# A macaron decoder layer in float32: two weight differences made by adding transfers, three pairs of k tiles by seven products, x in four pieces

## Chip, cores, metric

One core of one Trainium2 chip runs the whole layer for a sequence of 256 positions. The metric is the device time of one execution in microseconds, as a median over runs.

## What is computed

The layer is a feed-forward part, a token mixer (dilated and differential attention with two gates), and a second feed-forward part. The change touches the two feed-forward parts, which are alike:

```python
D_MODEL, SEQ, D_FF = 2048, 256, 5632

def swiglu(h, w_gate, w_up, w_down):
    return (jax.nn.silu(h @ w_gate) * (h @ w_up)) @ w_down

x = x + 0.5 * swiglu(rms_norm(x, ffn1_norm), ffn1_w_gate, ffn1_w_up, ffn1_w_down)
...
x = x + 0.5 * swiglu(rms_norm(x, ffn2_norm), ffn2_w_gate, ffn2_w_up, ffn2_w_down)
```

All inputs are float32, and so is the output.

## The kernel before, in words

**Three matmuls a product.** Every float32 factor is kept as two parts: hi, a rounded copy that ScalarE makes, and lo, the rest, that VectorE makes by a subtraction. A product of two factors is then three matmuls on TensorE: hi with hi, hi with lo, lo with hi (`three`, lines 139 to 144; in `linear`, lines 133 to 135). The activations stand on TensorE as 128 x 128 weights, and 512 columns of the layer's weight matrix stream past.

**From memory to TensorE.** Weights come in tiles of two k tiles by 512 columns (512 KB). SP's queue loads one into a slot `raw` (four slots, pool `wraw`). ScalarE then makes `w_hi` from it and VectorE makes `w_lo`, into one of five pairs of slots (pool `wspl`), to which the feed-forward parts add a sixth (`FFN_SPL`, pool `acth`). A raw slot comes free when both parts are made and no difference still needs it; a hi/lo pair comes free when TensorE has used it. The helper `parts` (line 98) makes both, on lines 102 and 103; `weight_groups` (line 106) does the same on lines 117 and 118 for all other matrices.

**Two chunks at once.** The hidden width of 5632 is cut into 11 chunks of 512 columns. The first is made by `linear`, gate and up one after the other. For each of the other ten, `two_chunks` (line 166) makes gate and up together, walking over eight pairs u of k tiles. For a plain pair it does eight products: two k tiles, two halves of the positions, two matrices. For the pairs in `WINO` (3 and 5) it does seven, by Winograd's form of Strassen's method on 2 x 2 blocks: activations on one side, and on the other b00, b10 (gate's two k tiles) and b01, b11 (up's two). The sums of activations come from `sums_of_x` (line 146), once for each feed-forward part. The differences of weights are made for each pair on VectorE, on lines 203, 204, 209 and 210: b01 - b00, b01 - b11, b11 - (b01 - b00), and b10 less the last. `t_a` and `t_b` hold them, and each is split into hi and lo like a raw tile. Eight PSUM banks hold the four results and the four products.

**After a call.** Adds on VectorE put the results together (lines 220 to 226), ScalarE applies SiLU (line 372), VectorE multiplies and transposes blocks of 32 x 32 (line 267), SP writes the blocks to memory and reads them back in another order (`moved`, line 272), and eight groups later ScalarE and VectorE split them into hi and lo (`ah` and `al`, lines 240 and 241) for the product with w_down.

**What sets the order.** A list `later` holds work to be done after so many groups of weights (`defer`, `tick`). Within that, the compiler's scheduler orders the instructions of each engine by what it thinks is ready; afterwards every engine, and SP's and POOL's queues of transfers, keeps to its order. `tc.issue_after(ins)` puts what follows behind `ins` on its engine.

**At the start.** x is loaded in eight pieces of 256 columns by `load_x` (line 330), each followed by transposes on TensorE and a split; the first chunk's weight tiles come between them. `table_loads` (line 469) brings small tables through POOL's queue: four for the gains of the heads (line 472), four for lambda (line 475), and the positions. It is deferred to group 34. `rsqrt_mean` (line 229) uses a power operation on POOL.

Of the kernel before, what the change touches and what calls it, by code (L numbers as in the profile page):

```python
# [11 lines left out]
F32 = mybir.dt.float32  # L12
# [7 lines left out]
P = 128  # L20
# [12 lines left out]
FFN_SPL = 1  # L33
WINO = (3, 5)
# [19 lines left out]
def hybrid_layer_kernel(ctx: ExitStack, tc: tile.TileContext, a: dict, out: bass.AP):  # L54
# [34 lines left out]
    wtmp = None  # L89
    spl_turn = itertools.count()  # L90
# [7 lines left out]
    def parts(src, n=GRP):  # L98

        nonlocal last_hi, last_lo  # L100
        hi, lo = split_tiles()
        last_hi = nc.scalar.activation(hi[:, :n], src, AF.Copy)  # L102
        last_lo = nc.vector.tensor_tensor(lo[:, :n], src, hi[:, :n].bitcast(F32), op=ALU.subtract)  # L103
        return hi, lo

    def weight_groups(w, n0, nk):

        nonlocal last_hi, last_lo
        for k0 in range(0, nk, GRP):
            raw = wraw.tile([P, GRP, CH], F32, name="raw")  # L110
            hi, lo = split_tiles()
            step = 1 if groups == 0 else GRP
            for g in range(0, GRP, step):
                ks = slice(g, g + step)
                nc.sync.dma_start(raw[:, ks], w[(k0 + g) * P:(k0 + g + step) * P, n0:n0 + CH]
                                  .rearrange("(k p) n -> p k n", p=P))
                last_hi = nc.scalar.activation(hi[:, ks], raw[:, ks], AF.Copy)  # L117
                last_lo = nc.vector.tensor_tensor(lo[:, ks], raw[:, ks], hi[:, ks].bitcast(F32), op=ALU.subtract)  # L118
            yield k0, hi, lo
# [26 lines left out]
    def sums_of_x(pool, pairs):  # L146
# [3 lines left out]
        for u in pairs:  # L150
            f = wtmp.tile([P, GRP, CH], F32, name="t_a")
# [14 lines left out]
    def two_chunks(j, cols, xh, xl, nk, sx, tmp):  # L166
# [15 lines left out]
        for u in range(nu):  # L182
            raw = []
            for w, n0 in cols:
                r = wraw.tile([P, GRP, CH], F32, name="raw")
                nc.sync.dma_start(r, w[2 * u * P:(2 * u + 2) * P, n0:n0 + CH].rearrange("(k p) n -> p k n", p=P))
                raw.append(r)
# [11 lines left out]
            part = lambda hl, k: (hl[0][:, k], hl[1][:, k])  # L199
            b = parts(raw[0])  # L200

            ta, tb = wtmp.tile([P, GRP, CH], F32, name="t_a"), wtmp.tile([P, GRP, CH], F32, name="t_b")
            nc.vector.tensor_tensor(ta[:, 0], raw[1][:, 0], raw[0][:, 0], op=ALU.subtract)
            nc.vector.tensor_tensor(ta[:, 1], raw[1][:, 0], raw[1][:, 1], op=ALU.subtract)
# [4 lines left out]
            nc.vector.tensor_tensor(tb[:, 0], raw[1][:, 1], ta[:, 0], op=ALU.subtract)  # L209
            nc.vector.tensor_tensor(tb[:, 1], raw[0][:, 1], tb[:, 0], op=ALU.subtract)  # L210
            tick()
            b = parts(ta)
            three(p5, sm(0), part(b, 0), st, sp)
            three(p7, sm(2), part(b, 1), st, sp)
            b = parts(tb)
# [12 lines left out]

    def rsqrt_mean(ss, n, cols):

        v = small.tile([P, cols], F32, name=f"rv{cols}")
        nc.vector.tensor_scalar(v, ss, 1.0 / n, EPS, op0=ALU.mult, op1=ALU.add)
        r = small.tile([P, cols], F32, name=f"rr{cols}")
        nc.gpsimd.tensor_tensor(r, v, mhalf[:, :cols], op=ALU.pow)
        return r
# [94 lines left out]
    def load_x(i):  # L330

        if i < KD // 2:
            cols = slice(i * 2 * P, (i + 1) * 2 * P)
            nc.sync.dma_start(xs[:, :, cols], xv[:, :, cols])
            to_kmajor([xs[:, t, cols] for t in range(NT)], xh, xl, 2 * i, g1)
# [11 lines left out]
    def ffn(wg, wu, wd, norm, done, ahead=None):  # L347
        nonlocal wtmp
        with tc.tile_pool(name="act", bufs=1) as apool, tc.tile_pool(name="actw", bufs=1) as aw, \
                tc.tile_pool(name="actb", bufs=1) as bp, tc.tile_pool(name="acts", bufs=1) as sxp, \  # L350
                tc.tile_pool(name="actt", bufs=1) as wt, tc.tile_pool(name="acth", bufs=FFN_SPL) as spl:
            wtmp = wt
            more_spl.append(spl)
# [27 lines left out]
            more_spl.clear()  # L381
# [87 lines left out]
    def table_loads():  # L469

# [374 lines left out]
```

## Time and profile before

| | us |
|---|---|
| median of 3 runs | 2135.52 (2135.37 to 2136.85) |
| the profiled execution | 2133.2 |
| its span, first to last instruction | 2131.4 |

TensorE's clock was granted at 0.999 of full speed on average. The page gives busy times of the engines as shares of the span. Matmuls are pipelined: one matmul's record runs on beside the next one's, so the price of a matmul is the step from one start to the next. Idle time of another engine costs nothing as long as TensorE is fed.

### The profile page before, as it was taken

How to read it: one execution, taken by the hardware profiler on the slowest of the kernel's cores; microseconds unless marked ns; L12 is line 12 of the kernel's file. 1: busy time of each engine (PE TensorE's matmuls, PEld its weight loads, DVE VectorE, ACT ScalarE, POOL GpSimd, SP SyncE). 2: the span in 40 equal slices, each digit the busy share in tenths (PEclk: the TensorE clock that was granted, in tenths of full speed). 3: DMA queues.
4: the chain of work that ended last, by engine and by line, in shares of the span. 5: the costliest groups of instructions: out<-in, count | busy, mean ns of one | idle time of the engine just before them, and what ended most of it. 6: DMA issues, size and time to landing. Idle time of an engine off the chain costs nothing.

```text
span 2131.4 us, 25439 instructions
## 1 busy us (share of the span) xinstructions
PE 2112.3 (99%) x9370; PEld 1744.8 (82%) x9370; DVE 1482.3 (70%) x1880; ACT 1063.4 (50%) x1297; POOL 48.9 (2%) x50
## 2 busy tenths in 40 slices
PE   8999999999999999999999999999999999999999
PEld 7878888888888888888888888888888888888887
DVE  6788864588876665767755556676888745788853
ACT  6454543355545554555555444454554533455532
POOL 0000000000000011011100000000000000000000
PEclk9999999999999999999999999999999999999999
DMA  8666675566677766666654567676766755667673
GB/s 262 199 200 217 225 241 194 168 220 230 212 238 256 237 200 227 228 214 215 196 191 158 185 228 243 226 234 189 228 216 217 254 191 187 198 212 231 228 244 121
DMA packets 241665, 456.26 MB, mean 214 GB/s; under 512 B 14162, under 2 KB 37252, under 8 KB 241284
## 3 DMA queue, kind: packets, MB, share of 16 engines
q1 hardware_dynamic: 241152, 454.09, 64.4%
q0 software_dynamic: 288, 0.53, 0.2%
q8 instruction: 73, 1.20, 0.2%
q14 instruction: 52, 0.43, 0.1%
q10 hardware_dynamic: 100, 0.03, 0.0%
HBM read 428.89 MB, written 25.69 MB: 213 GB/s over the span
## 4 chain that ended last, share of the span: by engine, by line
PE 75%; DVE 11%; DMA 10%; issue 2%; ACT 1%; SPq 0%; DVEq 0%; ACTq 0%
PE mm L133 19%; PE mm L134 19%; PE mm L135 19%; DMA raw<-in_ffn_w_up_dram 7%; DVE w_lo L103 6%; PE mm L143 2%; PE mm L144 2%; PE mm L142 2%; PE tr L143 2%; PE tr L144 2%; PE tr L142 2%; PE s L144 1%; PE s L143 1%; PE s L142 1%; DMA raw<-in_ffn_w_gate_dram 1%
## 5 line engine op out<-in xcount | busy, mean ns | idle before, releaser
L118 DVE TENSOR_TENSOR w_lo<-raw,w_hi 128x1024 fp32r<-128x1024 f32 (+1 forms) x449 | 543.3, 1218 | 379.1 <-ACT w_hi L117 377.2
L117 ACT ACTIVATE w_hi<-raw 128x1024 fp32r<-128x1024 f32 (+1 forms) x449 | 471.4, 1056 | 482.1 <-PE mm L135 400.8
L102 ACT ACTIVATE w_hi<-raw 128x1024 fp32r<-128x1024 f32 x320 | 316.4, 1003 | 222.9 <-DMA raw<-in_ffn_w_gate_dram 47.8
L103 DVE TENSOR_TENSOR w_lo<-raw,w_hi 128x1024 fp32r<-128x1024 f32 x320 | 361.9, 1150 | 71.0 <-ACT w_hi L102 69.7
L133 PE MATMUL mm<-w_hi,xh 128*128 128x512 f32 x864 | 339.4, 394 | 0.0
L134 PE MATMUL mm<-w_lo,xh 128*128 128x512 f32 x864 | 338.9, 393 | 0.0
L135 PE MATMUL mm<-w_hi,xl 128*128 128x512 f32 x864 | 336.4, 392 | 0.0
L133 PE MATMUL mm<-w_hi,ah 128*128 128x512 f32 x704 | 273.9, 389 | 1.8 <-DVE e L226 1.8
L135 PE MATMUL mm<-w_hi,al 128*128 128x512 f32 x704 | 273.9, 389 | 0.0
L134 PE MATMUL mm<-w_lo,ah 128*128 128x512 f32 x704 | 273.9, 389 | 0.0
L143 PE MATMUL mm<-w_lo,xh 128*128 128x512 f32 x540 | 210.6, 390 | 0.3 <-DVE w_lo L103 0.3
L144 PE MATMUL mm<-w_hi,xl 128*128 128x512 f32 x540 | 210.1, 389 | 0.0
L142 PE MATMUL mm<-w_hi,xh 128*128 128x512 f32 x540 | 209.4, 389 | 0.0
L135 PEld LDWEIGHTS mm<-w_hi,xl 128*128 128x128 f32 x864 | 162.6, 188 | 33.6
L134 PEld LDWEIGHTS mm<-w_lo,xh 128*128 128x128 f32 x864 | 162.8, 188 | 33.3
L133 PEld LDWEIGHTS mm<-w_hi,xh 128*128 128x128 f32 x864 | 162.7, 189 | 33.3
L133 PEld LDWEIGHTS mm<-w_hi,ah 128*128 128x128 f32 x704 | 132.2, 188 | 30.0 <-ACT w_hi L117 1.4
L135 PEld LDWEIGHTS mm<-w_hi,al 128*128 128x128 f32 x704 | 132.2, 188 | 27.7
L134 PEld LDWEIGHTS mm<-w_lo,ah 128*128 128x128 f32 x704 | 132.2, 188 | 27.2
L143 PEld LDWEIGHTS mm<-w_lo,xh 128*128 128x128 f32 x540 | 101.4, 188 | 22.9 <-DVE w_lo L103 1.9
L142 PEld LDWEIGHTS mm<-w_hi,xh 128*128 128x128 f32 x540 | 101.4, 188 | 21.1
L144 PEld LDWEIGHTS mm<-w_hi,xl 128*128 128x128 f32 x540 | 101.4, 188 | 20.9
(229 smaller groups left out, 2717.5 us busy)
## 6 DMA issues: line engine op xcount, KB each, us to landing
raw<-in_w_in_dram SPq DMA_DIRECT2D x184, 512.0 KB, 3.6
raw<-in_ffn_w_up_dram SPq DMA_DIRECT2D x176, 512.0 KB, 4.7
raw<-in_ffn_w_down_dram SPq DMA_DIRECT2D x176, 512.0 KB, 4.7
raw<-in_ffn_w_gate_dram SPq DMA_DIRECT2D x175, 512.0 KB, 4.5
blocks<-turned SPq DMA_DIRECT2D x41, 512.0 KB, 4.1
raw<-in_w_out_dram SPq DMA_DIRECT2D x32, 512.0 KB, 4.5
moved<-blocks SPq DMA_DIRECT2D x31, 512.0 KB, 4.7
raw<-in_w_diff_branch_dram SPq DMA_DIRECT2D x16, 512.0 KB, 4.8
```

The costliest lines, as they stand in the source:

```text
L102: last_hi = nc.scalar.activation(hi[:, :n], src, AF.Copy)
L103: last_lo = nc.vector.tensor_tensor(lo[:, :n], src, hi[:, :n].bitcast(F32), op=ALU.subtract)
L117: last_hi = nc.scalar.activation(hi[:, ks], raw[:, ks], AF.Copy)
L118: last_lo = nc.vector.tensor_tensor(lo[:, ks], raw[:, ks], hi[:, ks].bitcast(F32), op=ALU.subtract)
L133: nc.tensor.matmul(ps[t], xh[:, k, sl], hi[:, kk], start=k == 0, stop=False)
L134: nc.tensor.matmul(ps[t], xh[:, k, sl], lo[:, kk], start=False, stop=False)
L135: nc.tensor.matmul(ps[t], xl[:, k, sl], hi[:, kk], start=False, stop=k == nk - 1)
L142: nc.tensor.matmul(ps, h, wh, start=start, stop=False)
L143: nc.tensor.matmul(ps, h, wl, start=False, stop=False)
L144: nc.tensor.matmul(ps, l, wh, start=False, stop=stop)
```

## The change

- `WINO` becomes (2, 4, 5): three pairs of k tiles go by seven products.
- Two of the four weight differences, b01 - b00 and b01 - b11, are made without VectorE. ScalarE writes -b00 and -b11 into `t_a`, and two transfers from POOL's queue add the block b01 from memory in place. The block b01 has no other use, so up's first k tile is no longer loaded into a raw slot for those pairs.
- The other two differences are written over b00 and b10 in the raw slot of gate, whose hi and lo parts have been made by then. `t_b` is gone; `t_a` has two slots.
- The feed-forward parts have a fifth raw slot (`FFN_RAW`) in place of the sixth hi/lo pair. The sums of x use raw slots as scratch.
- x is loaded in four pieces, of 256, 256, 512 and 1024 columns.
- The small tables are loaded behind the latest power operation on POOL.

```diff
-FFN_SPL = 1
-WINO = (3, 5)
+FFN_SPL = 0
+FFN_RAW = 1
+WINO = (2, 4, 5)
...
+    def raw_tile():
+        pool = wraw
+        if more_raw and next(raw_turn) % (RAW_BUFS + FFN_RAW) >= RAW_BUFS:
+            pool = more_raw[0]
+        return pool.tile([P, GRP, CH], F32, name="raw")
...
-            for w, n0 in cols:
-                r = wraw.tile([P, GRP, CH], F32, name="raw")
-                nc.sync.dma_start(r, w[2 * u * P:(2 * u + 2) * P, n0:n0 + CH].rearrange("(k p) n -> p k n", p=P))
+            for i, (w, n0) in enumerate(cols):
+                r = raw_tile()
+                k = i if u in sx else 0
+                nc.sync.dma_start(r[:, k:], w[(2 * u + k) * P:(2 * u + 2) * P, n0:n0 + CH]
+                                  .rearrange("(k p) n -> p k n", p=P))
...
+            b00, b10, b11 = raw[0][:, 0], raw[0][:, 1], raw[1][:, 1]
+            w, n0 = cols[1]
+            ta = wtmp[0].tile([P, GRP, CH], F32, name="t_a")
+            for i, block in enumerate((b00, b11)):
+                nc.scalar.activation(ta[:, i], block, AF.Copy, scale=-1.0)
+                nc.gpsimd.dma_start(ta[:, i], w[2 * u * P:(2 * u + 1) * P, n0:n0 + CH], accum_op=ALU.add)
             b = parts(raw[0])
-
-            ta, tb = wtmp.tile([P, GRP, CH], F32, name="t_a"), wtmp.tile([P, GRP, CH], F32, name="t_b")
-            nc.vector.tensor_tensor(ta[:, 0], raw[1][:, 0], raw[0][:, 0], op=ALU.subtract)
-            nc.vector.tensor_tensor(ta[:, 1], raw[1][:, 0], raw[1][:, 1], op=ALU.subtract)
             three(p1, op(0, 0), part(b, 0), st, sp)
             three(c00, op(1, 0), part(b, 1), False, False)
             b = parts(raw[1][:, 1:], 1)
             three(c01, sm(3), part(b, 0), False, False)
-            nc.vector.tensor_tensor(tb[:, 0], raw[1][:, 1], ta[:, 0], op=ALU.subtract)
-            nc.vector.tensor_tensor(tb[:, 1], raw[0][:, 1], tb[:, 0], op=ALU.subtract)
             tick()
+            nc.vector.tensor_tensor(b00, b11, ta[:, 0], op=ALU.subtract)
+            nc.vector.tensor_tensor(b10, b10, b00, op=ALU.subtract)
             b = parts(ta)
             three(p5, sm(0), part(b, 0), st, sp)
             three(p7, sm(2), part(b, 1), st, sp)
-            b = parts(tb)
+            b = parts(raw[0])
...
         if i < KD // 2:
+            if i in (0, 1, 2, 4):
+                piece = slice(i * 2 * P, max(2 * i, 1) * 2 * P)
+                nc.sync.dma_start(xs[:, :, piece], xv[:, :, piece])
             cols = slice(i * 2 * P, (i + 1) * 2 * P)
-            nc.sync.dma_start(xs[:, :, cols], xv[:, :, cols])
...
     def table_loads():
+        with tc.issue_after(last_pow[-1].ins):
+            small_loads()
+
+    def small_loads():
```

## Rows read from the trace of the kernel before

**Rows 1.** The page: busy time, share of the span and instructions of each engine.
```profile
PE 2112.3 (99%) x9370; PEld 1744.8 (82%) x9370; DVE 1482.3 (70%) x1880; ACT 1063.4 (50%) x1297; POOL 48.9 (2%) x50
```

**Rows 2.** Windows of 50 us: busy by engine, granted clock, DMA share, GB/s.
```profile
core 0: us, PE busy (x) PEld busy (x) DVE busy (x) ACT busy (x) POOL busy (x), PEclk, DMA share, GB/s
0.00:50.00 50.00, 42.54 (x192) 35.00 (x193) 33.11 (x53) 33.38 (x58) 5.02 (x14) 1.00 0.80 260
100.00:150.00 50.00, 46.33 (x197) 37.79 (x196) 43.85 (x86) 27.90 (x33) 0.00 (x0) 0.97 0.66 212
150.00:200.00 50.00, 50.00 (x223) 41.40 (x222) 43.34 (x53) 27.46 (x32) 0.00 (x0) 1.00 0.67 214
200.00:250.00 50.00, 49.58 (x219) 40.53 (x218) 42.27 (x49) 24.53 (x27) 0.00 (x0) 1.00 0.67 221
250.00:300.00 50.00, 49.22 (x216) 39.99 (x215) 39.19 (x43) 26.96 (x30) 0.00 (x0) 1.00 0.73 246
550.00:600.00 50.00, 49.27 (x216) 39.98 (x215) 40.37 (x50) 25.44 (x29) 0.00 (x0) 1.00 0.64 214
1650.00:1700.00 50.00, 48.95 (x216) 40.26 (x215) 40.56 (x44) 26.04 (x29) 0.00 (x0) 1.00 0.74 249
1950.00:2000.00 50.00, 49.35 (x218) 40.29 (x217) 42.31 (x51) 27.24 (x32) 0.00 (x0) 1.00 0.65 212
```

**Rows 3.** Timeline of TensorE, first and last of 85 matmul starts: start, duration.
```profile
149.62 0.39 PE L142 MATMUL mm<-w_hi,xh 128*128 128x512 f32 x1
...
168.66 0.39 PE L142 MATMUL mm<-w_hi,xh 128*128 128x512 f32 x1
```

**Rows 4.** Groups of instructions: count, busy us, mean ns, idle before and its releaser.
```profile
L102 ACT ACTIVATE w_hi<-t_a 128x1024 fp32r<-128x1024 f32 x40 | 42.2, 1055 | 39.5 <-PE s L144 18.9 <-PE mm L144 18.9 <-ACT w_hi L102 1.0
L103 DVE TENSOR_TENSOR w_lo<-t_a,w_hi 128x1024 fp32r<-128x1024 f32 x40 | 48.6, 1215 | 3.7 <-ACT w_hi L102 3.7
L203 DVE TENSOR_TENSOR t_a<-raw 128x512 f32<-128x512 f32 x40 | 27.7, 692 | 82.1 <-DMA raw<-in_ffn_w_up_dram 82.1
L102 ACT ACTIVATE w_hi<-raw 128x512 fp32r<-128x512 f32 x40 | 24.9, 623 | 23.6 <-PE s L144 13.3 <-PE mm L144 9.1 <-DMA raw<-in_ffn_w_up_dram 1.0
...
L153 DVE TENSOR_TENSOR t_a<-xh,xl 128x512 f32<-128x512 f32 x4 | 2.7, 687 | 0.1
```

**Rows 5.** POOL's loads of line 475 (64 KB each): issue in ns, landing.
```profile
L475 POOL DMA_DIRECT2D junk<-in_diff_lq_dram x2: 538/564/589, 87.7 to 89.2; - x2
...
DMA to landing us min/median/max: 4.0/6.1/6.4
```

**Rows 6.** DMA issues: count, KB each, median us from issue to landing.
```profile
raw<-in_ffn_w_up_dram SPq DMA_DIRECT2D x176, 512.0 KB, 4.7
```

**Rows 7.** Timelines of VectorE and TensorE, pair 5 of one call.
```profile
166.13 0.69 DVE L203 TENSOR_TENSOR t_a<-raw 128x512 f32<-128x512 f32 x1 [2.85 <-DMA raw<-in_ffn_w_up_dram]
...
173.76 1.22 DVE L103 TENSOR_TENSOR w_lo<-t_a,w_hi 128x1024 fp32r<-128x1024 f32 x1
...
177.28 0.39 PE L143 MATMUL tr<-w_lo,sx_h 128*128 128x512 f32 x1
```

**Rows 8.** Windows of 10 us, columns as in rows 2.
```profile
0.00:10.00 10.00, 2.54 (x10) 2.10 (x11) 2.02 (x5) 3.15 (x6) 3.73 (x11) 1.00 0.75 218
10.00:20.00 10.00, 10.00 (x43) 8.07 (x43) 6.90 (x10) 6.96 (x11) 0.00 (x0) 1.00 1.07 375
80.00:90.00 10.00, 10.00 (x45) 8.26 (x45) 9.86 (x20) 5.67 (x7) 2.27 (x4) 1.00 0.75 220
```

**Rows 9.** Timeline of POOL: start, duration, and idle before with its releaser.
```profile
1.29 0.71 POOL L472 DMA_DIRECT2D qkg<-in_dil_q_norm_dram  x1 [0.34 <-issue]
...
87.73 0.59 POOL L475 DMA_DIRECT2D junk<-in_diff_lq_dram  x1 [46.57 <-DVE mask L431]
```

**Rows 10.** Timeline of TensorE at the start.
```profile
8.83 1.09 PE L253 MATMUL tr<-ident,xs 128*128 128x128 f32 x4 [3.32 <-DMA xs<-in_x_dram]
9.57 0.78 PE L133 MATMUL mm<-w_hi,xh 128*128 128x512 f32 x1
```

**Rows 11.** Waits: who for whom, us in total, times, longest.
```profile
ACT ah L240 <- DMA moved<-blocks: 107.9, 22, 8.5
...
PE tr L143 <- DVE w_lo L103: 5.2, 4, 3.7
```

More of the change, by code (lines that the diff above doesn't have):

```diff
@@ L88, in hybrid_layer_kernel @@
     more_spl = []
-    wtmp = None
-    spl_turn = itertools.count()
+    more_raw = []
+    wtmp = []
+    spl_turn, raw_turn = itertools.count(), itertools.count()
+    def raw_tile():
[3 more added lines that the diff above has]
+        return pool.tile([P, GRP, CH], F32, name="raw")
     def split_tiles():
@@ L109, in weight_groups @@
         for k0 in range(0, nk, GRP):
-            raw = wraw.tile([P, GRP, CH], F32, name="raw")
+            raw = raw_tile()
             hi, lo = split_tiles()
@@ L150, in sums_of_x @@
         for u in pairs:
-            f = wtmp.tile([P, GRP, CH], F32, name="t_a")
+            f = raw_tile()
             x, sm = f[:, 0].rearrange("p (k s) -> p k s", s=S), f[:, 1].rearrange("p (i m) -> p i m", m=P)
@@ L227, in two_chunks @@
         return (e, x), (u2, y)
+    last_pow = []
     def rsqrt_mean(ss, n, cols):
@@ L233, in rsqrt_mean @@
         r = small.tile([P, cols], F32, name=f"rr{cols}")
-        nc.gpsimd.tensor_tensor(r, v, mhalf[:, :cols], op=ALU.pow)
+        last_pow.append(nc.gpsimd.tensor_tensor(r, v, mhalf[:, :cols], op=ALU.pow))
         return r
@@ L347, in ffn @@
     def ffn(wg, wu, wd, norm, done, ahead=None):
-        nonlocal wtmp
         with tc.tile_pool(name="act", bufs=1) as apool, tc.tile_pool(name="actw", bufs=1) as aw, \
                 tc.tile_pool(name="actb", bufs=1) as bp, tc.tile_pool(name="acts", bufs=1) as sxp, \
-                tc.tile_pool(name="actt", bufs=1) as wt, tc.tile_pool(name="acth", bufs=FFN_SPL) as spl:
-            wtmp = wt
-            more_spl.append(spl)
+                tc.tile_pool(name="actt", bufs=FFN_RAW) as wt, tc.tile_pool(name="acth", bufs=2) as sums:
+            more_raw.append(wt)
+            wtmp.append(sums)
             ah = apool.tile([P, 4 * HALVES[0], S], F32R, name="ah")
@@ L380, in ffn @@
                     (done if half else part)(n, ps, bp)
-            more_spl.clear()
+            wtmp.clear()
+            more_raw.clear()
     def part(n, ps, _):
```

## Prediction

> **What bounds the kernel now.** I read the page's busy shares first. TensorE is busy for 2112.3 of 2131.4 us and VectorE is next with 1482.3 [rows 1], so the time is TensorE's unless something starves it. Next came the windows of 50 us. In the stretches where two column chunks are made at once, TensorE is full or within about 1 us of full at a granted clock of 1.00, while VectorE is busy for 42 to 43 of 50 us and ScalarE for 25 to 27 [rows 2]. VectorE is therefore close behind. The six stretches with idle time that I count lose 3.67 + 0.42 + 0.78 + 0.73 + 1.05 + 0.65 = 7.3 us [rows 2]. The timeline of TensorE gives the price of a product. From the start at 149.62 to the one at 168.66 there are 84 steps, so 19.04 / 84 = 0.2267 us a matmul; its duration of 0.39 overlaps the next one [rows 3]. I use starts, not durations.
>
> **The change, part by part.**
>
> *One more pair by seven products.* Both feed-forward parts call the two-chunk routine 10 times. A plain pair costs 8 products of 3 matmuls, the other kind 7, so the third pair removes 3 matmuls in each of 20 calls: 60 x 0.2267 = **13.6 us**. All of it lies on TensorE, so it comes off the end if TensorE stays fed. A call then takes 183 x 0.2267 = 41.5 us in place of 186 x 0.2267 = 42.2.
>
> *VectorE.* A pair with seven products had 4 subtractions (0.69) and lo parts of 3 x 1.22 + 0.68; it loses two subtractions: 7.1 becomes 5.7 us. A plain pair is 2 x 1.22 = 2.4 [rows 4]; the half-wide lo part is taken like a subtraction. A call goes from 2 x 7.1 + 6 x 2.4 = 28.6 to 3 x 5.7 + 5 x 2.4 = 29.1, so +0.5 us. The share of the window, 43.3 of 50, is 36.6 us a call; 37.1 of 41.5 still fits. Cost 0; cover 4.4 us a call.
>
> *ScalarE.* Two negations of 0.62 come in each such pair. A call goes from 2 x 3.8 + 6 x 2.1 to 3 x 5.0 + 5 x 2.1 with the hi parts of 1.06 and 0.62 [rows 4], +5 us. From 27.5 of 50, or 23 us a call, it rises to 28 of 41.5. Cost 0 as work; its order in the queue is a matter for the rivals.
>
> *The two accumulating transfers.* The page shows no transfer that adds. The nearest rows are POOL's four loads of 64 KB beside a running feed-forward stage: 0.54 to 0.59 us to issue (two of the four), 4.0 to 6.4 to land, median 6.1 [rows 5]. A plain load of 512 KB lands in 4.7 [rows 6], so size is not what sets these times, and I take 6.1. After the second raw tile has landed, the old path was two subtractions, 1.4 us. The new one is two negations and a landing: 1.2 + 6.1 - 1.4 = **6.0 us later**, between 3.9 and 6.3 with the ends of the row. Three things pay for that:
> 1. In the second such pair of the call that I followed, t_a's lo part ended at 173.76 + 1.22 = 174.98, and the first product with it began at 177.28: a lead of 2.3 us [rows 7].
> 2. VectorE stood waiting for that raw tile before its first subtraction, 82.1 us in 40 pairs, 2.05 a pair [rows 4]; at 166.13 it is 2.85 [rows 7]. No subtraction stands there now.
> 3. A fifth raw slot lets each load start one release earlier. With 16 loads in 41.5 us that is 2.6 us.
>
> Together 6.95 against 6.0: about 1 us to spare in a typical pair, less in some. I take new stalls of 0.1 us a call, **+2 us**. The lower end is a gain: VectorE's freed wait could remove the 7.3 us of present idle. The upper end is nothing of 2 and 3 being worth anything: 6.0 - 2.3 = 3.7 us a call, 74 us.
>
> *Traffic.* Such a pair moved four blocks of 256 KB; now three, and two by POOL: +0.25 MB in three pairs of a call, and twice that if the destination's reads count. Against 8.4 MB a call that is 9 to 18%. The DMA share of 0.67 [rows 2] goes to at most 0.80; the windows show 1.07 [rows 8]. Cost 0. SP issues the same number of raw loads, half as large where the block b01 is left out.
>
> *Slots.* The sixth hi/lo pair goes. Five plain tiles are 5 x 12 x 0.2267 = 13.6 us of products, far above the lead of 2.3, so the lead was not set by this. Cost 0 unless the two adjacent pairs 4 and 5 eat the lead; that belongs to the 2 us.
>
> *Sums of x.* One more pair of tiles in each feed-forward part, six VectorE instructions of at most 0.69 [rows 4], under 4.2 us, in a window with 17 us of VectorE idle [rows 2]. They borrow raw slots in turn. Cost 0.
>
> *Start.* TensorE loses 7.5 of the first 10 us [rows 8]. POOL's four wide loads ran from 1.29 us [rows 9], before the second piece of x, for which TensorE stood 3.32 us [rows 10]. They now follow the first norm's power operations. 256 KB at the window's 218 GB/s [rows 8] are 1.2 us. The x pieces from 4 on arrive as one transfer of 1 MB: at 375 GB/s 2.8 us where a quarter took 0.7, so up to 2.1 us of delay for tile 8 if it were needed at once; but it is needed only after eight k tiles. I take **-1.0**, ends -1.2 and +2.1. On POOL's queue the four later loads wait for the mask until 87.73, a wait of 46.6 us [rows 9]; first-call transfers queued behind them could cost up to that once. But POOL's order follows what is ready, as the loads at 1.29 show, though the code writes them for group 34. Cost 0.
>
> **Sum.** The profiled execution took 2133.2 us, span 2131.4 and 1.8 around it. 2133.2 - 13.6 + 2 - 1.0 = 2120.6. The median of the runs lies 2.3 above that execution, so **2123 us**. 0.2%, or 4.3 us, is about what a measurement can tell from no change. The saving of 14.6 is gone if a call loses 0.73 us.
>
> **Rivals.**
>
> *A, the forecast:* the transfers are covered in nearly every pair. Own range 2117 to 2131 (stalls from none to 0.5 us a call). Chance 0.52.
>
> *B, present stalls go too:* VectorE, no longer held by a late raw tile, keeps further ahead; 2123 - 2 - 7.3 = 2114. For it speaks that TensorE's named idle there is for lo parts [rows 11]. Chance 0.12.
>
> *C, a draw:* 0.5 to 0.95 us a call come back at the adjacent pairs, 2131 to 2140. Chance 0.13.
>
> *D, slower: ScalarE's queue.* ScalarE takes its work in order, and its split of the turned activations waits for a DMA, 107.9 us in 22 waits, 4.9 each [rows 11]. A negation that stands behind that wait starts its transfer 4.9 us late; with 1 us to spare TensorE loses 3.9. It decides from four calls of 20 (0.73 x 20 / 3.9). In half the calls it gives 2121 + 39 = 2160, in all 2199. For it speaks that the wait falls in the call's fourth or fifth pair, where pair 4's negations come; against it that they need no split slot, so they can stand as early as their data. Chance 0.20.
>
> *E, slower: descriptors.* VectorE is busy for 9.86 of the ten microseconds in which POOL issued its loads, and the issues still took 0.54 to 0.59 [rows 5, 8]. If POOL nevertheless had to wait out one lo part of 1.22 us for each of two transfers, 2.4 - 1.0 = 1.4 us a call, 2121 + 28 = 2149. Chance 0.03. The Trainium skill, page SBUF — State Buffer, section "SBUF: two separate sides", has a rule of this kind against the change: while VectorE runs a copy-like operation that uses both port pairs, GpSimd "cannot write the descriptors" of its transfers; by its figure, 620 ns grown to 3100, the estimate would be 2.5 us a transfer. These rows do not show such a delay.
>
> **How the numbers follow.** Faster by over 0.2% is A and B, 0.64; within it C, 0.13; slower D and E, 0.23. The range 2113 to 2148 holds A, B's near half, C, and D's mildest cases; about 0.2 lies outside. The likeliest case alone is 2117 to 2131.
>
> **What would show it.** Right: 60 fewer wide matmuls with an unchanged step of 0.227; TensorE idle under 10 us between 50 and 2100; the transfers landing 5 to 7 us after issue; t_a's hi part waiting for its transfer without TensorE waiting for the lo part. Wrong: TensorE waiting for lo parts of t_a or of the raw tile in pairs 4 and 5, in sums above 15 us; a landing above 8 us; negations behind ScalarE's wait for the turned blocks; first products later than 9.57 [rows 10].

## The result, and the profile after

The changed kernel takes **2217.64 us** (median, 2214.78 to 2221.84); beside it the kernel before took 2135.44. The ratio is 1.0383, with an interval of 1.0368 to 1.0398: 82 us slower, where 12 us faster was forecast and the range ended at 2148.

The page after has these busy times (columns as in [rows 1]), then queues of transfers (packets, MB, share of sixteen engines' span), then loads (count, KB each, median us from issue to landing):

```profile
PE 2143.1 (97%) x9310; PEld 1731.2 (78%) x9310; DVE 1501.8 (68%) x1892; ACT 1150.1 (52%) x1459; POOL 152.8 (7%) x170
...
q0 software_dynamic: 17568, 31.99, 9.2%
...
raw<-in_ffn_w_gate_dram SPq DMA_DIRECT2D x175, 512.0 KB, 5.3
t_a<-in_ffn_w_up_dram POOLq DMA_DIRECT2D x120, 256.0 KB, 5.3
```

In the kernel before, gate's loads landed sooner:

```profile
raw<-in_ffn_w_gate_dram SPq DMA_DIRECT2D x175, 512.0 KB, 4.5
```

The 60 matmuls are gone (9310 in place of 9370). VectorE and ScalarE did the work that was forecast, and neither is full. But TensorE is idle for 2220.1 - 2143.1 = 77.0 us of the span, where it was 2131.4 - 2112.3 = 19.1 [rows 1]. Its busy time rose as well, by 30.8 us, although 60 matmuls fewer are in it. Two things in the rows go that way: a matmul's record is 0.39 long against a step of 0.227, so each stall leaves a tail of 0.16 that counts as busy, and the granted clock fell after stalls (below). How the 30.8 divides between them was not separated.

The waits of the same execution (who for whom, us in total, times, longest) say what TensorE stood for:

```profile
ACT t_a L216 <- DMA raw<-in_ffn_w_gate_dram: 128.3, 47, 5.5
ACT ah L256 <- DMA moved<-blocks: 70.6, 21, 5.6
ACT w_hi L110 <- DMA t_a<-in_ffn_w_up_dram: 54.6, 20, 5.1
ACT t_a L216 <- DMA raw<-in_ffn_w_up_dram: 31.6, 16, 4.5
PE mm L150 <- ACT w_hi L110: 29.3, 43, 3.6
PE tr L150 <- ACT w_hi L110: 26.5, 27, 3.7
PE s L150 <- ACT w_hi L110: 6.3, 11, 0.6
```

TensorE waits for **hi** parts, so for ScalarE: 29.3 + 26.5 + 6.3 = 62.1 us in 81 waits. Before it was named idle for lo parts [rows 11]. ScalarE in turn stood 159.9 us in front of its negations (L216), waiting for raw tiles, and 54.6 us in front of hi parts, waiting for adding transfers. In [rows 4] the hi parts of t_a waited for TensorE itself (39.5 us), which costs nothing.

Windows of 50, 10 and 5 us (columns as in rows 2) show where. The first line is a stretch of products with w_down, which the change does not touch; the second and the last lie where two chunks are made at once, the third at the start.

```profile
350.00:400.00 50.00, 50.00 (x222) 41.42 (x221) 25.51 (x23) 19.10 (x18) 0.00 (x0) 1.00 0.57 195
500.00:550.00 50.00, 43.71 (x179) 33.63 (x178) 37.47 (x43) 27.75 (x34) 5.17 (x6) 0.97 0.74 206
...
0.00:10.00 10.00, 4.83 (x16) 3.80 (x17) 3.12 (x8) 5.17 (x9) 0.70 (x6) 1.00 0.75 244
...
545.00:550.00 5.00, 3.71 (x9) 2.70 (x10) 3.95 (x4) 4.48 (x5) 0.00 (x0) 0.71 0.52 111
```

All of the loss lies in the calls of `two_chunks`: by the starts of their matmuls in the two traces, the four stretches of five calls take 945.2 us in all, against 853.3 before, and the rest of the span 1274.9, against 1278.2. The start gained: TensorE is busy for 4.83 of the first 10 us, against 2.54 [rows 8].

One call shows how a stall is made. Timeline of all engines, pairs 2, 4 and 5 (start, duration, and in brackets the idle time before and its releaser):

```profile
520.42 0.86 POOL L217 DMA_DIRECT2D t_a<-in_ffn_w_up_dram  x1 [0.61 <-ACT t_a L216]
...
520.90 0.37 SPq L195 DMA_DIRECT2D raw<-in_ffn_w_gate_dram  x1
...
527.72 0.63 ACT L216 ACTIVATE t_a<-raw 128x512 f32<-128x512 f32 x1 [4.89 <-DMA raw<-in_ffn_w_gate_dram]
528.26 1.04 ACT L110 ACTIVATE w_hi<-t_a 128x1024 fp32r<-128x1024 f32 x1
...
532.37 1.23 DVE L111 TENSOR_TENSOR w_lo<-raw,w_hi 128x1024 fp32r<-128x1024 f32 x1 [1.21 <-ACT w_hi L110]
...
533.62 1.81 SPq L195 DMA_DIRECT2D raw<-in_ffn_w_up_dram  x2
...
539.78 0.63 ACT L216 ACTIVATE t_a<-raw 128x512 f32<-128x512 f32 x1 [2.20 <-DMA raw<-in_ffn_w_up_dram]
...
540.71 0.86 POOL L217 DMA_DIRECT2D t_a<-in_ffn_w_up_dram  x1 [6.69 <-ACT t_a L216]
...
544.97 1.06 ACT L110 ACTIVATE w_hi<-t_a 128x1024 fp32r<-128x1024 f32 x1 [3.51 <-DMA t_a<-in_ffn_w_up_dram]
...
546.07 0.74 PE L150 MATMUL mm<-w_hi,sx_h 128*128 128x512 f32 x2 [3.63 <-ACT w_hi L110]
...
547.61 0.63 PE L150 MATMUL s<-w_hi,xh 128*128 128x512 f32 x1
548.04 0.63 PE L151 MATMUL mm<-w_lo,sx_h 128*128 128x512 f32 x1
```

The adding transfer that was issued at 520.42, by the view of transfers (count, KB, us from the start of the issue to landing):

```profile
t_a<-in_ffn_w_up_dram POOLq DMA_DIRECT2D x1, 256.0 KB, 7.6
```

Pair 2's second adding transfer was issued at 520.42 and took 7.6 us, where the median is 5.3, so its data were there at 528.0; ScalarE split them at 528.26. Gate's raw tile for pair 4, loaded beside it from 520.90 on, was slow too: the negation that waited for it could start only at 527.72, after 4.89 us. This negation stood ahead of the split, but held it here for 0.2 us at the most. Elsewhere a negation does hold up a split: the data of one hi part had landed at 2066.5 (issued at 2061.61, 4.9 us to landing), while ScalarE stood until 2068.28 at the negation ahead of it. After 528.26 came VectorE's second difference, the next hi part and its lo part. That lo part ended at 533.60 and freed the raw slot, and at 533.62 SP could load up's tile for pair 4. Its negation, its adding transfer and its hi part came at 539.78, 540.71 and 544.97, and TensorE stood for 3.63 us. So this stall has two makers: transfers that land late, and a row of load, negation and transfer in which each waits for the one before. After that stall the matmul step is 548.04 - 547.61 = 0.43 instead of 0.227: the granted clock of 0.71 in 545 to 550 mixes full speed and half speed (2.4 and 1.2 GHz). This stall thus cost more than its own length.

### The profile page after: what moved, and what is told of

Same layout as the page of the kernel before. It is cut to its first block, busy times and chain, and to the rows that moved or that the text cites. A ratio compares the mean times of both kernels' runs of the same rounds, so it can differ in the third digit from the quotient of the medians.

```text
span 2220.1 us, 25966 instructions
## 1 busy us (share of the span) xinstructions
PE 2143.1 (97%) x9310; PEld 1731.2 (78%) x9310; DVE 1501.8 (68%) x1892; ACT 1150.1 (52%) x1459; POOL 152.8 (7%) x170
## 3 DMA queue, kind: packets, MB, share of 16 engines
q0 software_dynamic: 17568, 31.99, 9.2%
## 4 chain that ended last, share of the span: by engine, by line
PE 61%; DMA 19%; issue 7%; DVE 7%; ACT 5%; POOL 1%; ACTq 0%; DVEq 0%; SPq 0%; POOLq 0%
PE mm L141 18%; PE mm L142 18%; PE mm L143 18%; DMA t_a<-in_ffn_w_up_dram 7%; DMA raw<-in_ffn_w_gate_dram 5%; DVE w_lo L111 3%; ACT w_hi L110 3%; DMA moved<-blocks 3%; DMA raw<-in_ffn_w_up_dram 2%; DMA blocks<-turned 2%; DVE turned L283 1%; PE mm L150 1%; ACT t_a L216 1%; PE mm L151 1%; PE mm L152 1%
## 5 line engine op out<-in xcount | busy, mean ns | idle before, releaser
L126 DVE TENSOR_TENSOR w_lo<-raw,w_hi 128x1024 fp32r<-128x1024 f32 (+1 forms) x449 | 544.3, 1220 | 387.4 <-ACT w_hi L125 385.5
L125 ACT ACTIVATE w_hi<-raw 128x1024 fp32r<-128x1024 f32 (+1 forms) x449 | 471.8, 1057 | 492.7 <-PE mm L143 442.9
L111 DVE TENSOR_TENSOR w_lo<-raw,w_hi 128x1024 fp32r<-128x1024 f32 (+1 forms) x380 | 419.0, 1135 | 131.8 <-ACT w_hi L110 130.7
L110 ACT ACTIVATE w_hi<-raw 128x1024 fp32r<-128x1024 f32 (+1 forms) x380 | 356.7, 981 | 125.5 <-DVE raw L225 50.9
L141 PE MATMUL mm<-w_hi,xh 128*128 128x512 f32 x864 | 339.0, 394 | 0.0
L142 PE MATMUL mm<-w_lo,xh 128*128 128x512 f32 x864 | 338.8, 393 | 0.0
L143 PE MATMUL mm<-w_hi,xl 128*128 128x512 f32 x864 | 336.7, 393 | 0.0
L151 PE MATMUL mm<-w_lo,xh 128*128 128x512 f32 x490 | 191.3, 390 | 0.1
L152 PE MATMUL mm<-w_hi,xl 128*128 128x512 f32 x490 | 190.9, 390 | 0.0
L143 PEld LDWEIGHTS mm<-w_hi,xl 128*128 128x128 f32 x864 | 162.5, 188 | 33.9 <-DVE xl L260 0.3
L141 PEld LDWEIGHTS mm<-w_hi,xh 128*128 128x128 f32 x864 | 162.7, 189 | 33.6 <-ACT xh L259 0.2
L142 PEld LDWEIGHTS mm<-w_lo,xh 128*128 128x128 f32 x864 | 162.9, 189 | 33.2
L150 PE MATMUL mm<-w_hi,xh 128*128 128x512 f32 x490 | 181.7, 398 | 4.5 <-ACT w_hi L110 4.3
L217 POOL DMA_DIRECT2D t_a<-in_ffn_w_up_dram x120 | 104.0, 884 | 1094.5 <-ACT t_a L216 1007.6
L216 ACT ACTIVATE t_a<-raw 128x512 f32<-128x512 f32 x120 | 75.1, 626 | 160.8 <-DMA raw<-in_ffn_w_gate_dram 128.3
L150 PEld LDWEIGHTS mm<-w_hi,xh 128*128 128x128 f32 x490 | 92.7, 190 | 32.2 <-ACT w_hi L110 14.4
```

Source lines behind the costliest of these rows:

```text
L141: nc.tensor.matmul(ps[t], xh[:, k, sl], hi[:, kk], start=k == 0, stop=False)
L142: nc.tensor.matmul(ps[t], xh[:, k, sl], lo[:, kk], start=False, stop=False)
L143: nc.tensor.matmul(ps[t], xl[:, k, sl], hi[:, kk], start=False, stop=k == nk - 1)
L150: nc.tensor.matmul(ps, h, wh, start=start, stop=False)
L151: nc.tensor.matmul(ps, h, wl, start=False, stop=False)
L152: nc.tensor.matmul(ps, l, wh, start=False, stop=stop)
```

## The experiments

Unless said otherwise, an edit is made on the changed kernel. **Theory L** (lateness): data come late because a raw tile, a negation in ScalarE's order and a transfer now follow one another. **Theory O** (occupation): an adding transfer holds up the other transfers. **Theory W** (work): VectorE, ScalarE or the slots cannot carry three such pairs. In the recorded expectations theory 1 is L, theory 2 blames the slots or the adjacent pairs 4 and 5, theory 3 is the cost of adding itself, which O explains, and theory 4 is the part of L that lies in ScalarE's order.

The kernel before took 2132.6 to 2134.5 us beside these runs, and 2135.4 beside the changed kernel, so a difference of 2 or 3 us between versions says nothing.

### Differences back on VectorE, three pairs

```diff
-                k = i if u in sx else 0
+                k = 0
...
-                nc.scalar.activation(ta[:, i], block, AF.Copy, scale=-1.0)
-                nc.gpsimd.dma_start(ta[:, i], w[2 * u * P:(2 * u + 1) * P, n0:n0 + CH], accum_op=ALU.add)
+                nc.vector.tensor_tensor(ta[:, i], raw[1][:, 0], block, op=ALU.subtract)
```

> The changed kernel, but b01 - b00 and b01 - b11 are made on VectorE from a full raw tile again; negations and adding transfers are gone, while the pairs (2, 4, 5), five raw slots, five hi/lo pairs, the slots written over and the start stay. Theory 1 (the serial path raw tile, negation, transfer, split holds slots and starves TensorE): back to 2120 to 2140 us, held up only by VectorE, whose work rises by two subtractions of 0.69 us in 60 pairs. Theory 2 (five hi/lo pairs and the adjacent pairs 4 and 5 are at fault, not the transfers): stays above 2180.

Measured: 2174.76 us, ratio 1.0199 [1.0169, 1.0228]. This meets neither forecast (2120 to 2140, or above 2180). Three pairs are 41 us slower than the kernel before without a single adding transfer. The group of ScalarE's hi parts (columns as in rows 4) names VectorE as the late one:

```profile
L110 ACT ACTIVATE w_hi<-raw 128x1024 fp32r<-128x1024 f32 x320 | 322.2, 1052 | 289.9 <-DVE raw L224 166.9 <-DMA raw<-in_ffn_w_up_dram 30.8 <-PE s L152 23.9
```

The same pairs and slots cost nothing when these two subtractions go and the transfers copy (2132.06 us, below). So some relief for VectorE was needed for a third pair; the one chosen here costs 43 us more than none.

### Copying in place of adding, everything else the same

```diff
-                nc.gpsimd.dma_start(ta[:, i], w[2 * u * P:(2 * u + 1) * P, n0:n0 + CH], accum_op=ALU.add)
+                nc.gpsimd.dma_start(ta[:, i], w[2 * u * P:(2 * u + 1) * P, n0:n0 + CH])
```

> The changed kernel with the transfers from POOL copying b01 instead of adding it, still behind the negations; so b01 stands in t_a in place of the differences. Theory 1 (latency of the path): 2205 to 2225 us, as the changed kernel. Theory 3 (adding is what costs: slow packets, or the share of the DMA engines that they take): below 2180.

Measured: 2170.61 us, ratio 1.0179 [1.0141, 1.0217]: 47 us less than the changed kernel. Every engine has the same instructions in the same order in both, so these 47 us belong to the kind of 120 transfers. What differs in the transfers, first in the copying version, then in the changed one (the line of t_a with shortest, median and longest issue in ns, then landing, both from the view of the tile):

```profile
q0 software_dynamic: 9888, 31.99, 5.2%
...
L217 POOL DMA_DIRECT2D t_a<-in_ffn_w_up_dram x120: 536/537/599, 54.4 to 2037.1; - x120
...
DMA to landing us min/median/max: 2.9/3.7/7.6
```

```profile
L217 POOL DMA_DIRECT2D t_a<-in_ffn_w_up_dram x120: 856/862/1216, 54.5 to 2084.2; - x120
...
DMA to landing us min/median/max: 4.0/5.3/7.8
```

The bytes are the same (31.99 MB), but an adding transfer takes 144 packets where a copy takes 80 (17568 - 9888 = 7680, over 120 is 64 more; 9888 less the 288 of before, over 120, is 80). It issues in 0.86 instead of 0.54 us and lands 1.6 us later. ScalarE's hi parts wait 54.6 us for transfers into `t_a` where they add and 23.5 us where they copy, so some of the 47 us may be the lateness of their own data. The run does not say how much is that, and how much their hold on the engines.

### No negations

```diff
-            for i, block in enumerate((b00, b11)):
-                nc.scalar.activation(ta[:, i], block, AF.Copy, scale=-1.0)
-                nc.gpsimd.dma_start(ta[:, i], w[2 * u * P:(2 * u + 1) * P, n0:n0 + CH], accum_op=ALU.add)
+            for i, block in enumerate((b00, b11)):
+                nc.gpsimd.dma_start(ta[:, i], w[2 * u * P:(2 * u + 1) * P, n0:n0 + CH])
```

> As the copying variant, and the negations are left out too: the two transfers of a pair wait for no raw tile and can run ahead as soon as t_a has a slot. Theory 1: 2118 to 2135 us, since the transfers leave the path although all of them are still made. Theory 2 (slots, adjacent pairs): above 2180. Theory 3: far below the changed kernel as well, and no better than the copying variant.

Measured: 2132.06 us, ratio 0.9992 [0.9978, 1.0005]. With neither the adding nor the wait for raw tile and ScalarE the loss is gone; against the copying version that is 38.5 us. So adding carries a part of it and the negations ahead of it another. It is still no gain: the saved 13.6 us do not show.

### Two pairs instead of three

```diff
-WINO = (2, 4, 5)
+WINO = (3, 5)
```

> The changed kernel with the pairs (3, 5) as before, by transfers. Theory 1 with the loss spread over all pairs: 40 pairs lose 1.6 us each (the changed kernel's 82 + 14.6 us over 60 pairs), 2133 + 64 = about 2197 us. Theory 2 (the adjacent pairs): 2125 to 2145.

Measured: 2161.78 us, ratio 1.0138 [1.0108, 1.0167], between the two forecasts. Even at the old count of pairs, 40 pairs by adding transfers lose 28 us, 0.7 a pair, so the trouble is not made by the third pair alone. But the third pair adds 56 us more, although 60 matmuls go with it; no run here shows why it costs more than the first two together.

### The start alone, on the kernel before

```diff
...
+            if i in (0, 1, 2, 4):
+                piece = slice(i * 2 * P, max(2 * i, 1) * 2 * P)
+                nc.sync.dma_start(xs[:, :, piece], xv[:, :, piece])
             cols = slice(i * 2 * P, (i + 1) * 2 * P)
-            nc.sync.dma_start(xs[:, :, cols], xv[:, :, cols])
...
     def table_loads():
+        with tc.issue_after(last_pow[-1].ins):
+            small_loads()
...
```

> The kernel before with only the change at the start: x in four pieces, the small tables behind the power operation. The trace of the changed kernel begins its first product at 7.28 us instead of 9.57, so 2.3 us less than before: 2131 us. If the later pieces of x or the moved tables cost elsewhere: no change or slower.

Measured: 2131.65 us, ratio 0.9996 [0.9985, 1.0007]. Too little to tell from no change.

### A free negation

```diff
-            for i, block in enumerate((b00, b11)):
-                nc.scalar.activation(ta[:, i], block, AF.Copy, scale=-1.0)
+            for i in range(2):
+                other_data = xh[:, 0:2].bitcast(F32).rearrange("p k s -> p (k s)")
+                nc.scalar.activation(ta[:, i], other_data, AF.Copy, scale=-1.0)
```

> The changed kernel, but ScalarE negates a part of the activations that has long been there, not b00 and b11; the differences are therefore of other data. Adding transfers, their bytes, ScalarE's work and all slots stay; only the wait for the raw tile goes from the path. Theory 1 (serial path): 2120 to 2145 us, nearly all of the loss gone although the transfers still add. Theory 3 (adding itself costs, by its packets and its share of the DMA engines): 47 us of the loss stay, above 2165.

Measured: 2179.66 us, ratio 1.0221 [1.0201, 1.0241]. The same work stays on ScalarE and the transfers still add, but no negation waits for a raw tile: 38 us less than the changed kernel. Leaving the negations out took as much, 38.5 us, off the copying version. It is the wait for the raw tile ahead of the transfer, not ScalarE's 75 us of work, that makes up most of this part. With the transfers issued that early, ScalarE no longer waits for one of them, though they still add.

### Pairs further apart; negations in the order of the code

```diff
-WINO = (2, 4, 5)
+WINO = (1, 3, 6)
```

> The changed kernel with the pairs (1, 3, 6) in place of (2, 4, 5): no two adjacent. Theory 1: the path from raw tile to split is as long as before in each pair, 2195 to 2225 us. Theory 2 (adjacent pairs): below 2170.

```diff
-                nc.scalar.activation(ta[:, i], block, AF.Copy, scale=-1.0)
+                with tc.issue_after(last_hi.ins):
+                    nc.scalar.activation(ta[:, i], block, AF.Copy, scale=-1.0)
```

> The changed kernel, with each negation held behind the hi part written just before it, so that ScalarE cannot take it early and stand at it while a split is ready. Theory 4 (ScalarE stands at negations put too early: 160 us of waits for raw tiles at line 216): below 2190 us. Theory 1: no better than the changed kernel, 2210 to 2250, since the transfers start later.

Measured: 2231.66 us, ratio 1.0465 [1.0444, 1.0486], and 2292.66 us, ratio 1.0751 [1.0727, 1.0775]. Both are slower than theory 1 had forecast (2195 to 2225, and 2210 to 2250). Spacing does not help, so the two adjacent pairs are not the cause. Negations put behind the hi part written just before make it worse. In that run the waits show the other end of the same chain:

```profile
ACT w_hi L110 <- DMA t_a<-in_ffn_w_up_dram: 217.8, 44, 6.4
```

It was 54.6 in the changed kernel. Standing early, a negation blocks hi parts that are ready; standing late, it delays its own transfer.

### Adding without a wait, and its control

```diff
-            for i, block in enumerate((b00, b11)):
-                nc.scalar.activation(ta[:, i], block, AF.Copy, scale=-1.0)
+            for i in range(2):
+                nc.gpsimd.memset(ta[:, i], 0.0)
                 nc.gpsimd.dma_start(ta[:, i], w[2 * u * P:(2 * u + 1) * P, n0:n0 + CH], accum_op=ALU.add)
```

> The changed kernel with t_a set to zero by POOL in place of ScalarE's negations, so the transfers add b01 to zeros and t_a holds b01 in place of the differences. They still add, but wait for no raw tile and for nothing on ScalarE. So far copying in place of adding was worth 47 us, and leaving the negations out 38 more. If adding costs through the DMA engines (packets, share, slower raw loads): about 2132 + 47 = 2180 us. If it costs only by landing later on a path that something waits for: 2130 to 2145.

The control is the same without `accum_op`:

> POOL sets t_a to zero and then a transfer copies b01 into it. The order of instructions on every engine is that of the version that zeroes and then adds (2168.4 us); only the kind of the 120 transfers differs. If adding itself costs, this is near the version that copies without zeroing (2132.1), at 2132 to 2140. If the zeroing in POOL's order, half a microsecond ahead of each transfer, makes the data late, this stays near 2165. t_a holds b01 here, not the differences.

Measured: adding 2168.37 us, ratio 1.0159 [1.0115, 1.0204]; copying **2131.86 us**, ratio 0.9987 [0.9975, 0.9999]. Again the order of instructions is the same on every engine, and the kind of transfer alone makes 36.5 us, now without any raw tile or ScalarE ahead of it. The page of the copying control with ScalarE's waits for raw tiles, then those of the adding version:

```profile
q0 software_dynamic: 9888, 31.99, 4.7%
...
raw<-in_ffn_w_gate_dram SPq DMA_DIRECT2D x175, 512.0 KB, 4.7
raw<-in_ffn_w_up_dram SPq DMA_DIRECT2D x116, 512.0 KB, 4.6
t_a<-in_ffn_w_up_dram POOLq DMA_DIRECT2D x120, 256.0 KB, 3.8
...
ACT w_hi L110 <- DMA raw<-in_ffn_w_up_dram: 31.1, 20, 3.9
ACT w_hi L110 <- DMA raw<-in_ffn_w_gate_dram: 27.6, 21, 3.5
```

```profile
q0 software_dynamic: 17568, 31.99, 9.5%
...
raw<-in_ffn_w_gate_dram SPq DMA_DIRECT2D x175, 512.0 KB, 5.4
raw<-in_ffn_w_up_dram SPq DMA_DIRECT2D x116, 512.0 KB, 5.1
t_a<-in_ffn_w_up_dram POOLq DMA_DIRECT2D x120, 256.0 KB, 6.2
...
ACT w_hi L110 <- DMA raw<-in_ffn_w_gate_dram: 44.3, 22, 4.7
ACT w_hi L110 <- DMA raw<-in_ffn_w_up_dram: 41.1, 25, 6.1
```

The share of POOL's queue doubles: 0.095 x 2166.8 / 120 = 1.7 us of all sixteen engines for each adding transfer, 0.047 x 2130.9 / 120 = 0.8 for a copy. SP's loads of raw tiles, which do not add anything, land 0.5 to 0.7 us later. `t_a` itself lands 2.4 us later too, but that is not what is paid here: in neither trace does ScalarE or VectorE wait for a transfer into `t_a`. What grew is ScalarE's waits for raw tiles, from 58.7 to 85.4 us. That is theory O.

### Idle transfers: occupation or lateness

The base is the version without negations. An unread tile takes extra transfers. The first attempt had two for each pair:

```diff
...
+            for i in range(2):
+                nc.gpsimd.dma_start(idle[0], w[2 * u * P:(2 * u + 1) * P, n0:n0 + CH], accum_op=ALU.add)
...
```

> Base: the version whose transfers copy b01 and whose negations are left out (2132.1 us; t_a holds b01 itself). Added: one more tile of 256 KB that nothing reads, zeroed once, and behind the two copies of each seven-product pair two more transfers from POOL's queue that ADD b01 into that tile: 120 adding transfers on which nothing waits but the next such transfer. If adding costs by what it occupies (transfer engines, packets, the other transfers' time), this is 30 us or more above 2132, near the 2168 of the version that adds without waiting for ScalarE, with raw tiles landing in 5 us or more. If adding costs only because its data arrive later, it stays within 8 us of the run with 120 idle copies. That run tells what the extra traffic alone costs.

> The same as the run with idle adding transfers, but the 120 extra transfers copy b01 into the unread tile in place of adding it. Instructions and bytes are the same; only the kind of the idle transfers differs. If extra traffic of 31 MB on POOL's queue is what costs, this is 10 to 30 us above 2132 and the adding version as much or a little more. If it is adding itself that occupies, this stays within 8 us of 2132 and only the adding version is slower. If only lateness counts, both stay near 2132.

Measured: adding 2220.13 us, ratio 1.0422 [1.0401, 1.0444]; copying 2155.93 us, ratio 1.0111 [1.0096, 1.0126]. This pair settles little. The idle transfers waited for each other on POOL (555.5 and 442.1 us in all) and stood between the copies of t_a, which were up to 21.6 us late for ScalarE in the adding run, up to 10.5 in the copying run.

In the second attempt there is one idle transfer for each pair, fixed behind the two copies in POOL's order:

```diff
-                nc.gpsimd.dma_start(ta[:, i], w[2 * u * P:(2 * u + 1) * P, n0:n0 + CH])
+                copy = nc.gpsimd.dma_start(ta[:, i], w[2 * u * P:(2 * u + 1) * P, n0:n0 + CH])
+            with tc.issue_after(copy.ins):
+                nc.gpsimd.dma_start(idle[0], w[2 * u * P:(2 * u + 1) * P, n0:n0 + CH], accum_op=ALU.add)
...
```

> Base: the version that copies b01 into t_a without negations (2132.1 us; t_a holds b01). Behind the two copies of each seven-product pair, in POOL's order, one more transfer of 256 KB adds b01 into a tile that nothing reads: 60 adding transfers that cannot run ahead or bunch up. If adding costs by what it occupies, half of 36 us comes back: 2146 to 2155. If adding costs because its own data are late, no more than the run with 60 idle copies, within 4 us.

> The same as the run with 60 idle adding transfers, in the same order, but the extra transfers copy. If extra traffic on POOL's queue costs by its bytes (15.7 MB), 2137 to 2145. If it does not, 2130 to 2135, and the idle adding run beside it shows what adding occupies.

Measured: adding **2155.12 us**, ratio 1.0099 [1.0082, 1.0115]; copying **2141.35 us**, ratio 1.0035 [1.0022, 1.0048]. The idle copies then the idle adds, by their pages:

```profile
q0 software_dynamic: 14688, 47.72, 7.0%
...
raw<-in_ffn_w_gate_dram SPq DMA_DIRECT2D x175, 512.0 KB, 4.8
t_a<-in_ffn_w_up_dram POOLq DMA_DIRECT2D x120, 256.0 KB, 4.2
```

```profile
q0 software_dynamic: 18528, 47.72, 9.7%
...
raw<-in_ffn_w_gate_dram SPq DMA_DIRECT2D x175, 512.0 KB, 5.2
t_a<-in_ffn_w_up_dram POOLq DMA_DIRECT2D x120, 256.0 KB, 4.7
```

Nobody reads the idle tile; only the next idle transfer could wait for one, and it did so for 16.4 us in all, on POOL (14.2 with copies). In neither trace does ScalarE or VectorE wait for a transfer into `t_a`. Sixty copies cost 9 us over the base, and turning them into adds, with every engine's order unchanged, costs 13.8 us more. In proportion, 120 would cost 28 of the 36.5 us (an estimate). An adding transfer thus holds up the other transfers: gate's raw tiles and `t_a` come later, though they only copy. Theory O holds for the price of adding where nothing stands waiting for the sum itself.

### Other places for the work, and another slot

```diff
-                nc.scalar.activation(ta[:, i], block, AF.Copy, scale=-1.0)
+                nc.gpsimd.tensor_scalar(ta[:, i], block, -1.0, None, op0=ALU.mult)
```

> The changed kernel with the negations on POOL instead of ScalarE; the path from raw tile to split keeps its links. Theory 4 (ScalarE's order: the negations stand in it for raw tiles and make the splits late): below 2190 us. Theory 1 (the length of the path): 2205 to 2240.

```diff
-                k = i if u in sx else 0
+                k = 0
...
-                nc.scalar.activation(ta[:, i], block, AF.Copy, scale=-1.0)
-                nc.gpsimd.dma_start(ta[:, i], w[2 * u * P:(2 * u + 1) * P, n0:n0 + CH], accum_op=ALU.add)
+                nc.gpsimd.tensor_tensor(ta[:, i], raw[1][:, 0], block, op=ALU.subtract)
```

> The changed kernel with both differences by subtractions on POOL from a full raw tile: no negation, no adding transfer, no load on VectorE or ScalarE. If a subtraction takes POOL under 2 us and VectorE is not held up: 2118 to 2135 us, a version that could beat both. If the two engines hold each other up, VectorE's times rise above 1.22 us a lo part and the time is above 2150.

```diff
-FFN_RAW = 1
+FFN_RAW = 2
...
-tc.tile_pool(name="acth", bufs=2) as sums
+tc.tile_pool(name="acth", bufs=1) as sums
```

> The changed kernel with a sixth raw slot, paid with the second slot of t_a. Theory 2, narrowed to raw slots (a pair's gate tile is held until its last split, so the next loads start late): below 2195 us. Theory 1: within 15 us of the changed kernel; if two t_a slots matter, slower.

Measured: negations on POOL 2261.93 us, ratio 1.0597 [1.0551, 1.0644]; differences on POOL, with up's tile loaded whole, 2182.22 us, ratio 1.0224 [1.0178, 1.027]; a sixth raw slot, paid for with t_a's second slot, 2222.6 us, ratio 1.0413 [1.0359, 1.0467]. The first lies above both forecasts. A negation on POOL takes 1.64 us (median), not 0.63, in a chain that is late already: ScalarE no longer stands at negations, but its hi parts wait 181.1 us for the adding transfers, against 54.6 in the changed kernel. The last run gives no sign that raw slots are short, but it changed two things at once. For the differences on POOL, the views of t_a and of w_lo's lines (shortest, median, longest in ns):

```profile
L216 POOL TENSOR_TENSOR t_a<-raw x120: 1280/1724/2762, 56.4 to 2044.2; 128x512 f32<-128x512 f32 x120
...
L111 DVE TENSOR_TENSOR w_lo<-t_a,w_hi x60: 1172/1218/2314, 65.1 to 2052.3; 128x1024 fp32r<-128x1024 f32 x60
```

POOL and VectorE stretch each other: a subtraction on POOL takes up to 2.76 us, VectorE's lo part up to 2.31, where it never passed 1.23 us in the changed kernel. The Trainium skill, page SBUF — State Buffer, section "Who interferes with whom", says that a VectorE instruction with two SBUF inputs contends with a GpSimd instruction that reads SBUF; these rows agree.

### The new slots with two pairs on VectorE

```diff
-WINO = (2, 4, 5)
+WINO = (3, 5)
...
-                k = i if u in sx else 0
+                k = 0
...
-                nc.scalar.activation(ta[:, i], block, AF.Copy, scale=-1.0)
-                nc.gpsimd.dma_start(ta[:, i], w[2 * u * P:(2 * u + 1) * P, n0:n0 + CH], accum_op=ALU.add)
+                nc.vector.tensor_tensor(ta[:, i], raw[1][:, 0], block, op=ALU.subtract)
```

> The change's slots and start, but two pairs (3 and 5) by seven products with all four differences on VectorE, as before the change; up's tile is loaded whole. What differs from the kernel before: the differences from the third on are written over gate's raw slot, a fifth raw slot in place of the sixth hi/lo pair, x in four pieces, tables later. If the new slots cost nothing, 2130 to 2134, as the kernel before with the start alone (2131.7); if they free the loads and take the 19 us of idle time of TensorE away, 2120 to 2128; if overwriting gate's raw slot holds loads back, 2136 to 2150.

Measured: 2133.78 us, ratio 1.0004 [0.9995, 1.0014]. Taken together with the new start, the fifth raw slot for the sixth hi/lo pair and the differences written over gate's raw slot cost nothing and bring nothing. TensorE is idle for 17.3 us of the span, 19.1 before.

## Why the prediction was wrong, point by point

Put in a row, the runs take the 86 us between the changed kernel and the copying control apart. 2217.6 becomes 2179.7 when the negation waits for no raw tile (-38.0), 2168.4 when it leaves ScalarE altogether (-11.3), and 2131.9 when the transfer copies (-36.5). By another way: 2217.6, 2170.6 when it copies (-47.0), 2132.1 without the negations (-38.5). Adding is worth 36 to 47 us, and the negations ahead of it, mostly by their wait for raw tiles, 38 to 49, whichever goes first. Of these steps the two to copying, 36.5 and 47.0, compare kernels with the same order of instructions; in the others the scheduler also ordered some work anew.

- **Matmuls: right.** 60 went, and between two stalls the step is still 0.227.
- **VectorE and ScalarE as work: right.** VectorE rose by 19.5 us and ScalarE by 86.7; neither is the bound.
- **The step that failed first: "Together 6.95 against 6.0: about 1 us to spare in a typical pair", and the 2 us made from it.** The median landing was on the safe side, 5.3 us for 6.1, but the longest took 7.8 where the row had ended at 6.4 [rows 5]. The covers were not there. VectorE's former wait of 2.05 a pair [rows 4] and the fifth raw slot were counted as time saved. The slot brought nothing (2133.78 us with the new slots and two pairs on VectorE), and the new chain runs through ScalarE, not VectorE: ScalarE stands 159.9 us for raw tiles ahead of the negations, and a slot is freed by the last lo part of the pair before, so a late pair makes the next load late. Without the wait ahead of the transfers the kernel is 38 us faster. The forecast's upper end named this case, with covers 2 and 3 worth nothing, at 74 us; it was then left out of the range. The kernel lost more than that, 97 us (82 and the 14.6 not saved), because the next step failed as well.
- **The step that failed second: "Traffic ... Cost 0".** It counted bytes, and even twice the bytes for the destination's reads, and compared the sum with a share that peaks at 1.07 [rows 8]. The share came out as forecast, 0.74 in 500 to 550 where at most 0.80 was expected; what failed is that this costs nothing. An adding transfer took 144 packets for 80 and held the sixteen engines for 1.7 us in place of 0.8, so raw tiles landed later. The price is 36 to 47 us.
- **The start: right, and under-sized.** The first products came at 7.28 (the first row below) instead of 9.57 [rows 10], 2.3 us earlier; -1.0 was taken. As a change by itself it is too small to be measured.
- **Rival D: right engine, wrong wait.** ScalarE's order does matter, but the wait for the turned blocks fell from 107.9 [rows 11] to 70.6 us. It is the raw tiles that the negations wait for, 63 of 120 of them.
- **Rival E: did not come.** In the copying version the issues took 0.536 to 0.599 us beside a VectorE that is busy 69% of the time. Adding raises the shortest issue to 0.856, so it is the kind of transfer and not a starved POOL.
- **What was to be seen if it was wrong:** lo parts were named as what TensorE would wait for, and a landing above 8 us. TensorE waits for hi parts, and the longest landing was 7.8.
- **Rivals B and C:** even at an ideal price, with transfers that copy and wait for nothing, the kernel ends at 2131.9, 9 us above the forecast of 2123. So the forecast would have been missed by 9 us even without the two failed steps. There ScalarE waits 111.5 us in 45 cases for VectorE's second difference (the second row below), against 48.7 us in 16 cases with two pairs on VectorE. That the third pair gives most of its 13.6 us back there is likely, but no run here took that wait away.

```profile
7.28 1.20 PE L141 MATMUL mm<-w_hi,xh 128*128 128x512 f32 x2
...
ACT w_hi L110 <- DVE raw L225: 111.5, 45, 4.8
```

No version here beats the kernel before: those that compute the layer and lie nearest are the start alone (0.9996) and the new slots with two pairs on VectorE (1.0004), and both intervals hold 1.

## What to carry to other kernels

A transfer that adds in place is not a copy with free arithmetic: price it by the share that its queue takes of the transfer engines, by making the same kernel copy instead of add, since that leaves every instruction where it was. A saving that puts a load, an engine and a second transfer in a row before a product must be covered by what that chain's last engine has to spare, on its in-order queue; time that another engine used to wait was no cover here. When an upper bound comes from covers that nothing in the trace shows at work, it belongs in the range.

## What the runs showed of the hardware

- An adding transfer of 256 KB from POOL's queue takes 144 packets, 0.86 us to issue and 5.3 us to land in the changed kernel; a copy in the same place 80 packets, 0.54 and 3.7 us. Of the sixteen engines' time the adding transfer takes 1.7 us, the copy 0.8 (without negations).
- Sixty adding transfers that nobody reads slow the kernel by 13.8 us more than sixty copies of the same bytes, with the instructions of every engine in the same order.
- A subtraction of 128 x 512 on POOL takes 1.72 us (median) beside a busy VectorE, whose own operations stretch to nearly twice their length; on VectorE it took 0.69 [rows 4].
- After one stall of 3.6 us TensorE's step was 0.43 us in place of 0.227, and the granted clock of that 5 us stretch was 0.71 of full speed.
